# Side products held back in VectorE's queue, a fourth held weight chunk, and a hand-written end in a one-core transformer layer

## Chip, cores and metric

The kernel runs on one core of one Trainium2 chip, as one launch. The metric is the device time of an execution in microseconds (us), lower is better; of several runs the median counts.

## What is computed

One layer of a decoder trunk for 256 tokens of width 2048, all in float32. From the reference, cut to what matters here:

```python
mod = c_act @ w_mod[l] + b_mod[l]                    # one vector of 12288 per sequence
sh1, sc1, g1, sh2, sc2, g2 = jnp.split(mod, 6, axis=-1)
h = _rms_norm(x, mix_norm_pre[l]) * (1.0 + sc1[:, None]) + sh1[:, None]
y = _token_mixer(h, ...)                             # attention + gated linear attention, then @ w_out
x = x + g1[:, None] * _rms_norm(y, mix_norm_post[l])
h = _rms_norm(x, ffn_norm_pre[l]) * (1.0 + sc2[:, None]) + sh2[:, None]
y = _conv_ffn(h, ...)                                # w_up, causal convolution, gate, w_down
x = x + g2[:, None] * _rms_norm(y, ffn_norm_post[l])
```

`w_mod` is 2048 x 12288; it multiplies a single vector, so it is not a matmul of TensorE here but 96 x 2 multiply-and-sum passes of VectorE over tiles of 128 x 1024.

## The kernel before, in words

**Weights.** Every weight matrix is streamed once through SBUF in parts of 128 x 1024 float32 (512 KB). For each part q the program does four steps: `load` (SyncE starts the DMA into one of 4 `raw` buffers, four parts ahead), `prep` (ScalarE rounds `raw` into `hi`, L272; VectorE subtracts, `lo = raw - hi`, L276; three buffers of each), and three parts later the matmuls on `hi` and `lo` (`mm3` at L292 to L294, or the pair at L343). The product with `lo` keeps float32 accuracy, so TensorE cannot pass a part before VectorE's subtraction of it. I call L276 the subtraction.

**Side products.** The rows of `w_mod`, and the shift's share of the first projections, come through a second set of buffers, `auxb` (three, later two of 128 x 1024). `aux_load` (L239) starts their DMA on the same SyncE queue; `aux_proc` hands the tile to `mod_proc` (L207, one multiply-and-sum on VectorE, and a small L211 after each second one) or to `bias_proc`. The first 64 halves (`N_EARLY`) use other buffers. `aux_step` walks a list of due places, `pos`, and issues both.

**Order.** TensorE and SyncE run in the order in which the program is written (`manual_schedule` over the whole kernel). On VectorE, ScalarE and GpSimd a scheduler sets the order by its own estimate of when each instruction could start, except inside further `manual_schedule` blocks, where the order is the written one. So where a side product stands among the subtractions is the scheduler's choice.

**Output projection.** `outer_mm` keeps eight accumulators, two token halves t by four column blocks n, over 16 chunks c. With `split`, the last three chunks are multiplied for t = 0 first and their weights kept (`hold`, regions H and C), then for t = 1; so the norm of t = 0 runs beside the matmuls of t = 1. At a place in that second pass `mid` calls `h2_first`: the matmuls with a diagonal matrix (`h2_mm`, L1027) that transpose and scale x for the next layer half, and their evacuation. At the very end `evac_out` does the same for t = 1, with 52 dummy matmuls (`keep_warm`, L1020) while the chain of t = 1 runs: squares, sum and power -0.5 (`rstd4`, L940 and L941), the residual add (`out_x1`, L1000), squares again, `rstd4`, the diagonal (L120).

**End.** `evac_y2` finishes the second down projection: per block an add from PSUM (L1125), a square on ScalarE (L1126), the product with the gate row (L1120, on GpSimd for the first blocks, on VectorE for the others), and after the fourth block `rstd4` and four final multiply-adds (L1134), each with its output DMA (L1136).

Of the kernel before, what the change touches and what calls it, by code (L numbers as in the profile page):

```python
# [38 lines left out]
def block_kernel(ctx: ExitStack, tc: tile.TileContext, x, cvec, pos, idn, cst, vec, vec2, gmask,  # L39
# [190 lines left out]
    def aux_load(i):  # L230
# [24 lines left out]
    def prep(it, half, defer=False):  # L255
# [13 lines left out]
        else:  # L269
# [30 lines left out]
    def outer_mm(c, n_all, x_of, evac, split=False, mid=None):  # L300
# [13 lines left out]
        def go(it, half, hi, lo):  # L314
            if not split or c < n_all - 3:
                for n in (2 * half, 2 * half + 1):
                    for t in range(2):
                        one(c, t, n, hi, lo)
                return
# [3 lines left out]
            if c == n_all - 1 and half == 1:  # L323
                cs_ = range(n_all - 3, n_all)
# [619 lines left out]
    def evac_out(t, n, ps):  # L944
# [6 lines left out]
        if t == 0 or n < 3:  # L951
            out_sums(n, ps)
        if n < 3:
            return
        if t == 0:
            out_x1(0, rstd4(S["ss4"]))
            S["dg", 0] = diag_of(rstd4(S["ssx"]))
            return

        with tc.manual_schedule(engines={ET.DVE, ET.Activation}):  # L960
            out_sums(3, ps)
            up_lo = S["prep_up"]()
            h2_act(0, 2)
            rs = rstd4(S["ss4"])
            out_x1(1, rs)
            h2_act(0, 3)
            rs = rstd4(S["ssx"])
            h2_shift(0, 2)
            S["dg", 1] = diag_of(rs)
            h2_split(0, 2)  # L970
            h2_shift(0, 3)
            keep_warm()
            for n in range(4):
                h2_mm(1, n)
            h2_act(1, 0, range(1))
            h2_split(1, 0, range(1))
            h2_act(1, 0, range(1, 3))
            h2_shift(1, 0)
            h2_split(1, 0, range(1, 4))
            for n in range(1, 4):  # L980
                h2_act(1, n, range(4))
                h2_split(1, n)
                if n == 1:
                    up_lo()
                if n == 2:
                    h2_split(0, 3)
            S["prep_up"]()()

    def out_sums(n, ps):
        nc.scalar.activation(sqj, ps, AF.Square, accum_out=S["ss4"][:, n:n + 1])  # L990
        yg = t2k()
# [12 lines left out]
    def h2_first():  # L1004
# [6 lines left out]
        for n in range(2):  # L1011
            h2_act(0, n)
            h2_shift(0, n)
            h2_split(0, n)

    def keep_warm():

        wm = bank(4)
        for _ in range(52):
# [25 lines left out]
    def h2_split(t, n, js=range(4)):  # L1045
# [4 lines left out]
        nc.vector.tensor_copy(hh, ht)  # L1050
        nc.vector.tensor_tensor(hl, ht, hh.bitcast(F32), op=ALU.subtract)  # L1051
# [60 lines left out]
    def evac_y2(t, n, ps):  # L1112
        if n == 0:
            S["ss4"] = small(4, "ss4")
            S["yg"] = []
        y1 = S["y1"][:, t]

        def gate(m):
# [3 lines left out]
            S["yg"].append(yg)  # L1122
# [4 lines left out]
        gate(n)  # L1127
        if n < 3:
            return
        rs = rstd4(S["ss4"])  # L1130
        for n in range(4):
            ns = slice(n * 512, (n + 1) * 512)
            y = y1[:, ns]
            nc.vector.scalar_tensor_tensor(out=y, in0=S["yg"][n], scalar=rs, in1=S["x1"][:, t, ns], op0=ALU.mult,  # L1134
                                           op1=ALU.add)
            nc.sync.dma_start(out=out[t * P:(t + 1) * P, ns], in_=y)  # L1136
# [148 lines left out]
```

## Time and profile before

| what | value |
|---|---|
| median of 3 runs | 1598.68 us (1593.10, 1598.68, 1600.93) |
| the profiled execution's own time | 1597.75 us |
| its span, first to last instruction | 1595.6 us |
| TensorE busy | 1563.3 us, 98% |
| VectorE busy | 1222.5 us, 77% |
| ScalarE busy | 825.7 us, 52% |
| GpSimd busy | 17.0 us, 1% |
| mean granted TensorE clock | 0.997 |
| DMA | 403 MB, mean 253 GB/s |

The profiled execution's time is its span and 2.15 us around it. A matmul's end in the records is modelled and matmuls overlap, so TensorE's "busy" is an upper bound; its idle time between matmuls is what the views of waits show.

### The profile page before, as it was taken

Reading aid. Unit: us, or ns where it says so; the run is one execution under the profiler, and the core shown is the slowest. Engines: PE = TensorE matmul, PEld = TensorE weight load, DVE = VectorE, ACT = ScalarE, POOL = GpSimd, SP = SyncE. Lnnn points to the kernel's source line nnn. Section 1 sums busy time; section 2 is a strip of 40 time slices with the busy share of each in tenths; the row PEclk is TensorE's granted clock in tenths of the full one; section 3 lists DMA queues with packets and bytes.
Section 4 is the critical chain, followed back from the end, with each engine's and each line's share of the span. In section 5 each row is a group of like instructions: output and inputs, shape, how many; then the busy total and the mean of one; then the engine's idle time right before and its main releaser. Section 6 shows DMA issues by size and latency. Waiting matters only on the chain.

```text
span 1595.6 us, 21287 instructions
## 1 busy us (share of the span) xinstructions
PE 1563.3 (98%) x7752; PEld 1293.2 (81%) x7752; DVE 1222.5 (77%) x1869; ACT 825.7 (52%) x1221; POOL 17.0 (1%) x35
## 2 busy tenths in 40 slices
PE   8999999999999999999999999999999999999997
PEld 6878888877767788777888888888778888888886
DVE  7999989968977778877778877777546777776446
ACT  5455565544477544443366555555335555555333
POOL 0000000000000000000000000000000000000001
PEclk9999999999999999999999999999999999999999
DMA  9999987877777799889935667677665555555554
GB/s 367 382 352 410 360 274 257 277 273 256 250 244 263 257 306 326 293 293 314 354 133 199 230 231 238 217 245 231 231 224 187 182 185 185 186 186 189 194 197 132
DMA packets 154841, 403.18 MB, mean 253 GB/s; under 512 B 12720, under 2 KB 70704, under 8 KB 154480
## 3 DMA queue, kind: packets, MB, share of 16 engines
q1 hardware_dynamic: 154736, 401.82, 72.9%
q8 instruction: 61, 1.00, 0.3%
q14 instruction: 44, 0.36, 0.1%
HBM read 399.68 MB, written 2.10 MB: 252 GB/s over the span
## 4 chain that ended last, share of the span: by engine, by line
PE 31%; DMA 22%; DVE 13%; issue 5%; ACT 2%; SPq 1%; POOL 0%; DVEq 0%; POOLq 0%; ACTq 0%
DMA aux<-in_wM_dram 21%; PE ps L343 16%; DVE lo L276 6%; PE ps L293 5%; PE ps L294 5%; PE ps L292 5%; DVE aux L207 2%; DMA raw<-in_wO_dram 1%; ACT hi L272 1%; SPq L251 0%; DVE aux L348 0%; DVE t2k L742 0%; DVE t2k L1093 0%; DVE y L1134 0%; SPq L253 0%
## 5 line engine op out<-in xcount | busy, mean ns | idle before, releaser
L272 ACT CAST hi<-raw 128x1024 fp32r<-128x1024 f32 x520 | 544.9, 1050 | 476.1 <-PE ps L294 366.9
L276 DVE TENSOR_TENSOR lo<-raw,hi 128x1024 fp32r<-128x1024 f32 x518 | 629.2, 1221 | 142.0 <-ACT hi L272 139.6
L343 PE MATMUL ps<-h,hi 128*128 128x512 f32 x1664 | 582.0, 398 | 1.0 <-DVE h L1051 1.0
L343 PE MATMUL ps<-h,lo 128*128 128x256 f32 x1664 | 451.0, 281 | 1.0 <-DVE lo L276 0.9
L343 PEld LDWEIGHTS ps<-h,hi 128*128 128x128 f32 x1664 | 306.4, 188 | 69.2 <-issue 1.3
L343 PEld LDWEIGHTS ps<-h,lo 128*128 128x128 f32 x1664 | 314.0, 189 | 13.8 <-DVE lo L276 4.4
L207 DVE SCALAR_TENSOR_TENSOR aux<-aux,cact 128x1024 f32<-128x1024 f32 x128 | 156.4, 1223 | 145.7 <-DMA aux<-in_wM_dram 145.6
L292 PE MATMUL ps<-hi,h 128*128 128x512 f32 x608 | 240.0, 395 | 1.6 <-ACT h L297 1.1
L293 PE MATMUL ps<-lo,h 128*128 128x512 f32 x608 | 237.4, 391 | 2.6 <-DVE lo L276 2.5
L294 PE MATMUL ps<-hi,h 128*128 128x512 f32 x608 | 237.1, 390 | 1.5 <-DVE h L298 0.8
L293 PEld LDWEIGHTS ps<-lo,h 128*128 128x128 f32 x608 | 114.2, 188 | 29.2 <-DVE lo L276 4.9
L294 PEld LDWEIGHTS ps<-hi,h 128*128 128x128 f32 x608 | 114.1, 188 | 26.9 <-DVE h L298 1.2
L292 PEld LDWEIGHTS ps<-hi,h 128*128 128x128 f32 x608 | 114.2, 188 | 26.7 <-ACT h L297 1.5
L293 PE MATMUL ps<-lo,act_ab 128*128 128x512 f32 x256 | 100.3, 392 | 2.2 <-DVE lo L276 2.2
L294 PE MATMUL ps<-hi,act_ab 128*128 128x512 f32 x256 | 99.7, 389 | 0.0
L292 PE MATMUL ps<-hi,act_ab 128*128 128x512 f32 x256 | 99.7, 389 | 0.0
L207 DVE SCALAR_TENSOR_TENSOR early<-early,cact 128x1024 f32<-128x1024 f32 x64 | 78.0, 1218 | 1.3 <-ACT cact L143 1.3
L347 ACT ACTIVATE aux<-ps 128x256 f32<-128x256 f32 x88 | 33.5, 380 | 75.4 <-PE ps L343 75.2
L1090 ACT ACTIVATE t2k<-aux,vc 128x256 f32<-128x256 f32 x88 | 52.8, 601 | 26.6 <-DVE aux L348 26.4
L348 DVE SCALAR_TENSOR_TENSOR aux<-ps,aux 128x256 f32<-128x256 f32 x88 | 37.0, 421 | 35.6 <-ACT aux L347 35.6
L293 PEld LDWEIGHTS ps<-lo,act_ab 128*128 128x128 f32 x256 | 48.0, 188 | 14.4 <-DVE lo L276 4.6
L292 PEld LDWEIGHTS ps<-hi,act_ab 128*128 128x128 f32 x256 | 48.0, 188 | 10.1
(270 smaller groups left out, 1614.2 us busy)
## 6 DMA issues: line engine op xcount, KB each, us to landing
raw<-in_wU_dram SPq DMA_DIRECT2D x176, 512.0 KB, 3.8
aux<-in_wM_dram SPq DMA_DIRECT2D x128, 512.0 KB, 6.0
raw<-in_wD_dram SPq DMA_DIRECT2D x88, 512.0 KB, 3.9
early<-in_wM_dram SPq DMA_DIRECT2D x64, 512.0 KB, 6.7
raw<-in_wS_dram SPq DMA_DIRECT2D x32, 512.0 KB, 6.4
raw<-in_wOG_dram SPq DMA_DIRECT2D x32, 512.0 KB, 7.0
aux<-in_wS_dram SPq DMA_DIRECT2D x32, 512.0 KB, 5.7
raw<-in_wQK_dram SPq DMA_DIRECT2D x32, 512.0 KB, 5.4
```

The costliest lines, as they stand in the source:

```text
L207: nc.vector.scalar_tensor_tensor(out=raw, in0=raw, scalar=1.0, in1=cact[:, half * HW:(half + 1) * HW], op0=ALU.mult, op1=ALU.mult, accum_o ...
L272: nc.scalar.copy(hi[:, :w], raw)
L276: nc.vector.tensor_tensor(lo[:, :w], raw, hi[:, :w].bitcast(F32), op=ALU.subtract)
L292: nc.tensor.matmul(out=o, lhsT=lh, rhs=rh, start=start, stop=False)
L293: nc.tensor.matmul(out=o, lhsT=lh, rhs=rl, start=False, stop=False)
L294: nc.tensor.matmul(out=o, lhsT=ll, rhs=rh, start=False, stop=stop)
L343: nc.tensor.matmul(out=o, lhsT=w, rhs=m, start=c == 0 and o is ps, stop=c == nk - 1 and o is ps)
L347: nc.scalar.activation(o, ps[:, TOK:], AF.Copy, scale=scale)
L348: nc.vector.scalar_tensor_tensor(out=o, in0=ps[:, :TOK], scalar=scale, in1=o, op0=ALU.mult, op1=ALU.add)
L1090: nc.scalar.activation(z, u, AF.Identity, scale=w2, bias=vc2[:, W_CB + f:W_CB + f + 1])
```

## The change

Four edits; no arithmetic is added or taken away except six more dummy matmuls.

1. A side product beyond the first 64 is tied, by `tc.issue_after`, behind a subtraction on VectorE's queue: that of part lq + 3, where lq is the step at which the product's DMA was issued. That is the last weight part whose DMA stands ahead of the product's on SyncE's queue. It is an order on one engine's queue, without a semaphore.
2. The output projection holds its last four chunks instead of three; `mid` comes before the first block of the last chunk instead of before its third.
3. Behind `mid`, all of VectorE's and ScalarE's work up to the feed-forward layer is in written order, and that order is another: the four squares first, three gate products, the sum, the fourth gate product; `keep_warm` has 58 matmuls and writes bank 0 instead of 4.
4. The whole of `evac_y2` is in written order on VectorE, ScalarE and GpSimd: the four final multiply-adds of t = 0 are put between the blocks of t = 1 (one after block 0, one after block 1, two after block 2).

```diff
@@ aux_load, aux_proc
-        a["raw"] = raw
+        a["raw"], a["lq"] = raw, S.get("q", 0)
...
     def aux_proc(i):
         a = aux[i]
-        (mod_proc if a["kind"] == "mod" else bias_proc)(a, a["half"], a.pop("raw"))
+        go = mod_proc if a["kind"] == "mod" else bias_proc
+        if i < N_EARLY:
+            return go(a, a["half"], a.pop("raw"))
+
+        with tc.issue_after(los[max(k for k in los if k <= a["lq"] + LAG)]):
+            go(a, a["half"], a.pop("raw"))
@@ prep
-            nc.vector.tensor_tensor(lo[:, :w], raw, hi[:, :w].bitcast(F32), op=ALU.subtract)
+            los[it["q"] + half] = nc.vector.tensor_tensor(lo[:, :w], raw, hi[:, :w].bitcast(F32), op=ALU.subtract).ins
...
+    LAG, los = 3, {}
@@ outer_mm
-            if not split or c < n_all - 3:
+            if c < n_all - split:
...
-                    if n == 2 and c_ == n_all - 1 and mid:
+                    if n == 0 and c_ == n_all - 1 and mid:
                         mid()
@@ evac_out, t == 1
-        with tc.manual_schedule(engines={ET.DVE, ET.Activation}):
-            out_sums(3, ps)
-            up_lo = S["prep_up"]()
-            h2_act(0, 2)
-            rs = rstd4(S["ss4"])
-            out_x1(1, rs)
...
+        o = [S["o1", i] for i in range(4)]
+        for i in range(4):
+            out_square(i, o[i])
+        for i in range(3):
+            out_gate(i, o[i])
+        rs = rstd4(S["ss4"])
+        out_gate(3, o[3])
+        h2_act(0, 3)
+        out_x1(1, rs)
+        up_lo = S["prep_up"]()
...
@@ keep_warm
-        wm = bank(4)
-        for _ in range(52):
+        wm = bank(0)
+        for _ in range(58):
@@ items of wO
-        w_item(wO[c], D, outer_mm(c, KC, mg_of, evac_out, True, h2_first),
-               hold={KC - 3: ("H", True, 0), KC - 2: ("C", True, 0)}.get(c))
+        w_item(wO[c], D, outer_mm(c, KC, mg_of, evac_out, 4, h2_first),
+               hold={KC - 4: ("H", True, 0), KC - 3: ("H", False, 4), KC - 2: ("C", True, 0)}.get(c))
@@ evac_y2
+        if t == 0 and n == 0:
+            S["end"] = ExitStack()
+            S["end"].enter_context(tc.manual_schedule(engines={ET.DVE, ET.Activation, ET.Pool}))
+            S["out"] = []
...
         gate(n)
+        if t:
+
+            for _ in range((1, 1, 2, 0)[n]):
+                S["out"].pop(0)()
         if n < 3:
             return
         rs = rstd4(S["ss4"])
...
+        for m in range(4):
+            if t:
+                finish(m, rs)
+            else:
+                S["out"].append(lambda m=m: finish(m, rs))
```

Three places of the order show it. In these rows "aux" with its number is a side buffer, "macc" the product's sum, "lo<-raw,hi" a subtraction.

VectorE, where the first up projection ends and the first down projection begins; before:

```order
L298 TENSOR_TENSOR act_c<-t2k,act_c 128x256
L276 TENSOR_TENSOR lo<-raw,hi 128x1024 x2
L207 SCALAR_TENSOR_TENSOR aux_103,macc<-aux_103,cact 128x1024
L211 SCALAR_TENSOR_TENSOR modc<-macc,vc 128x1
L276 TENSOR_TENSOR lo<-raw,hi 128x1024 x4
L207 SCALAR_TENSOR_TENSOR aux_102,macc<-aux_102,cact 128x1024
```

and with the change:

```order
L304 TENSOR_TENSOR act_c<-t2k,act_c 128x256
L281 TENSOR_TENSOR lo<-raw,hi 128x1024
L207 SCALAR_TENSOR_TENSOR aux_102,macc<-aux_102,cact 128x1024
L281 TENSOR_TENSOR lo<-raw,hi 128x1024 x4
L207 SCALAR_TENSOR_TENSOR aux_103,macc<-aux_103,cact 128x1024
L211 SCALAR_TENSOR_TENSOR modc<-macc,vc 128x1
L281 TENSOR_TENSOR lo<-raw,hi 128x1024 x4
L207 SCALAR_TENSOR_TENSOR aux_102,macc<-aux_102,cact 128x1024
```

Each product stands two subtractions later. Counted over the whole program, 121 of the 160 side products that are tied stood, before, ahead of the subtraction of the last weight part requested before their own data; with the change none does.

VectorE, second unit of the sliding-window attention (dn is the softmax's denominator, es the sink's share, oa the attention's output); before:

```order
L276 TENSOR_TENSOR lo<-raw,hi 128x1024
L207 SCALAR_TENSOR_TENSOR aux_104,macc<-aux_104,cact 128x1024
L211 SCALAR_TENSOR_TENSOR modc<-macc,vc 128x1
L207 SCALAR_TENSOR_TENSOR aux_102,macc<-aux_102,cact 128x1024
L756 TENSOR_TENSOR dn<-dn,es 128x4
L757 RECIPROCAL dn<-dn 128x4
L207 SCALAR_TENSOR_TENSOR aux_103,macc<-aux_103,cact 128x1024
```

and with the change:

```order
L281 TENSOR_TENSOR lo<-raw,hi 128x1024
L207 SCALAR_TENSOR_TENSOR aux_102,macc<-aux_102,cact 128x1024
L207 SCALAR_TENSOR_TENSOR aux_103,macc<-aux_103,cact 128x1024
L211 SCALAR_TENSOR_TENSOR modc<-macc,vc 128x1
L762 TENSOR_TENSOR dn<-dn,es 128x4
L763 RECIPROCAL dn<-dn 128x4
L281 TENSOR_TENSOR lo<-raw,hi 128x1024 x2
```

Two products stand between the subtraction and dn in both, but not the same two: counted from the program's start, 121 side products stand ahead of this dn before, and 119 with the change. The 121st, of aux_102 right ahead of dn in the first excerpt, now comes after it.

VectorE, end of the program (y the down projection's output, x the residual); before:

```order
L1125 TENSOR_TENSOR y_10322<-ps_12722,y_10322 128x512
L1134 SCALAR_TENSOR_TENSOR y_10322<-t2k,r4r,x_6867 128x512 x4
L1125 TENSOR_TENSOR y_10322<-ps_12730,y_10322 128x512
L1125 TENSOR_TENSOR y_10322<-ps_12744,y_10322 128x512
L1125 TENSOR_TENSOR y_10322<-ps_12752,y_10322 128x512
L1120 TENSOR_TENSOR t2k<-y_10322,row 128x512
```

and with the change:

```order
L1162 TENSOR_TENSOR y_10324<-ps_12724,y_10324 128x512
L1157 SCALAR_TENSOR_TENSOR y_10324<-t2k,r4r,x_6851 128x512
L1162 TENSOR_TENSOR y_10324<-ps_12732,y_10324 128x512
L1157 SCALAR_TENSOR_TENSOR y_10324<-t2k,r4r,x_6851 128x512
L1162 TENSOR_TENSOR y_10324<-ps_12746,y_10324 128x512
L1157 SCALAR_TENSOR_TENSOR y_10324<-t2k,r4r,x_6851 128x512 x2
L1162 TENSOR_TENSOR y_10324<-ps_12754,y_10324 128x512
L1151 TENSOR_TENSOR t2k<-y_10324,row 128x512
```

The four final multiply-adds of t = 0 no longer stand in one block ahead of three of the four adds of t = 1, but between them.

## Rows read from the trace of the kernel before

**Rows 1.** Head of the page and its part 1.

```profile
span 1595.6 us, 21287 instructions
...
PE 1563.3 (98%) x7752; PEld 1293.2 (81%) x7752; DVE 1222.5 (77%) x1869; ACT 825.7 (52%) x1221; POOL 17.0 (1%) x35
```

**Rows 2.** TensorE's groups by line: xcount | busy us, mean ns | idle before, releasers.

```profile
L343 PE MATMUL ps<-h,lo 128*128 128x256 f32 x1664 | 451.0, 281 | 1.0 <-DVE lo L276 0.9
...
L293 PE MATMUL ps<-lo,h 128*128 128x512 f32 x608 | 237.4, 391 | 2.6 <-DVE lo L276 2.5
...
L293 PE MATMUL ps<-lo,act_ab 128*128 128x512 f32 x256 | 100.3, 392 | 2.2 <-DVE lo L276 2.2
...
L293 PE MATMUL ps<-lo,ob 128*128 128x512 f32 x128 | 50.2, 393 | 1.3 <-DVE lo L276 1.3
...
L293 PE MATMUL ps<-lo,mg 128*128 128x512 f32 x112 | 43.9, 392 | 0.8 <-DVE lo L276 0.8
...
L293 PE MATMUL ps<-lo,oa 128*128 128x512 f32 x64 | 25.3, 396 | 0.5 <-DVE lo L276 0.5
...
L783 PE MATMUL ps<-t2k,qkv 128*64 128x256 f32 (+1 forms) x40 | 8.2, 454 | 2.4 <-ACT t2k L772 2.4
```

**Rows 3.** Waits, all engines: us in total, times, longest.

```profile
DVE aux L207 <- DMA aux<-in_wM_dram: 145.6, 87, 4.5
```

**Rows 4.** VectorE's timeline, first down projection: start, us, line, idle before.

```profile
1120.42 1.23 DVE L207 SCALAR_TENSOR_TENSOR aux<-aux,cact 128x1024 f32<-128x1024 f32 x1 [4.49 <-DMA aux<-in_wM_dram]
...
1121.57 2.35 DVE L276 TENSOR_TENSOR lo<-raw,hi 128x1024 fp32r<-128x1024 f32 x2
```

**Rows 5.** TensorE's timeline there.

```profile
1122.85 0.50 PE L293 MATMUL ps<-lo,act_ab 128*128 128x512 f32 x1 [0.87 <-DVE lo L276]
```

**Rows 6.** VectorE's timeline, second unit of the attention.

```profile
467.04 1.22 DVE L207 SCALAR_TENSOR_TENSOR aux<-aux,cact 128x1024 f32<-128x1024 f32 x1 [3.30 <-DMA aux<-in_wM_dram]
...
468.19 0.16 DVE L756 TENSOR_TENSOR dn<-dn,es 128x4 f32<-128x4 f32 x1
```

**Rows 7.** ScalarE's timeline there.

```profile
466.56 0.60 ACT L834 ACTIVATE tb<-ps 128x512 f32<-128x512 f32 x1
...
468.66 1.70 ACT L760 ACTIVATE t2k<-t2k,dn 128x256 f32<-128x256 f32 x4 [1.50 <-DVE dn L757]
...
470.27 0.56 ACT L772 COPY t2k<-ps 128x512 f32<-128x512 f32 x1
```

**Rows 8.** Windows around it: busy by engine, granted clock (PEclk), DMA share, GB/s.

```profile
467.00:475.00 8.00, 5.62 (x19) 2.23 (x17) 5.90 (x10) 6.04 (x11) 0.00 (x0) 0.79 0.36 129
```

**Rows 9.** TensorE's timeline, end of the output projection.

```profile
823.50 3.84 PE L1027 MATMUL ps<-diag,x 128*128 128x128 f32 x32 [0.58 <-DVE diag L120]
...
828.56 6.38 PE L1020 MATMUL ps<-mg 128*128 128x256 f32 x52
...
836.12 3.81 PE L1027 MATMUL ps<-diag,x 128*128 128x128 f32 x32 [1.18 <-DVE diag L120]
...
843.48 0.47 PE L343 MATMUL ps<-h,hi 128*128 128x512 f32 x1 [0.61 <-DVE h L1051]
...
845.51 0.50 PE L343 MATMUL ps<-h,hi 128*128 128x512 f32 x1 [0.41 <-DVE h L1051]
```

**Rows 10.** VectorE's timeline, end of the program.

```profile
1580.91 3.84 DVE L1134 SCALAR_TENSOR_TENSOR y<-t2k,r4r,x 128x512 f32<-128x512 f32 x4
...
1586.58 0.72 DVE L1120 TENSOR_TENSOR t2k<-y,row 128x512 f32<-128x512 f32 x1
...
1588.96 2.74 DVE L1134 SCALAR_TENSOR_TENSOR y<-t2k,r4r,x 128x512 f32<-128x512 f32 x4 [1.09 <-POOL r4r L941]
```

**Rows 11.** GpSimd's timeline there.

```profile
1580.93 1.29 POOL L1120 TENSOR_TENSOR t2k<-y,row 128x512 f32<-128x512 f32 x1
...
1585.49 2.94 POOL L1120 TENSOR_TENSOR t2k<-y,row 128x512 f32<-128x512 f32 x2 [3.27 <-DVE y L1125]
...
1588.38 0.54 POOL L941 TENSOR_TENSOR r4r<-r4m,mhalf 128x1 f32<-128x1 f32 x1
```

More of the change, by code (lines that the diff above doesn't have):

```diff
@@ L298, in split_to, with outer_mm @@
         nc.vector.tensor_tensor(lo_ap, src_ap, hi_ap.bitcast(F32), op=ALU.subtract)
-    def outer_mm(c, n_all, x_of, evac, split=False, mid=None):
+    def outer_mm(c, n_all, x_of, evac, split=0, mid=None):
         def one(c, t, n, hi, lo):
@@ L323, in go @@
             if c == n_all - 1 and half == 1:
-                cs_ = range(n_all - 3, n_all)
+                cs_ = range(n_all - split, n_all)
                 for c_, n in [(c_, n) for c_ in cs_ for n in range(4)] if mid else [(c_, n) for n in range(4) for c_ in cs_]:
-                    if n == 2 and c_ == n_all - 1 and mid:
+                    if n == 0 and c_ == n_all - 1 and mid:
                         mid()
@@ new lines, in evac_out @@
+        keep_warm()
+        for n in range(4):
+            h2_mm(1, n)
+        up_lo()
+        h2_act(1, 0, range(1))
+        h2_split(1, 0, range(1))
+        h2_act(1, 0, range(1, 3))
+        h2_act(1, 0, range(3, 4))
+        h2_split(1, 0, range(1, 4))
+        h2_act(1, 1)
+        h2_shift(1, 1)
+        h2_split(1, 1)
+        up_lo = S["prep_up"]()
+        h2_act(1, 2, range(4))
+        h2_split(1, 2)
+        h2_act(1, 3)
+        h2_shift(1, 3)
+        h2_split(1, 3)
+        up_lo()
@@ L990, in out_sums, with out_square, out_gate @@
+        S["gap"].close()
+    def out_square(n, ps):
         nc.scalar.activation(sqj, ps, AF.Square, accum_out=S["ss4"][:, n:n + 1])
+    def out_gate(n, ps):
         yg = t2k()
@@ L1010, in h2_first @@
             h2_mm(0, n)
-        for n in range(2):
+        S["gap"] = ExitStack()
+        S["gap"].enter_context(tc.manual_schedule(engines={ET.DVE, ET.Activation}))
+        for n in range(3):
             h2_act(0, n)
             h2_shift(0, n)
-            h2_split(0, n)
+            if n < 2:
+                h2_split(0, n)
     def keep_warm():
-        wm = bank(4)
-        for _ in range(52):
+        wm = bank(0)
+        for _ in range(58):
             nc.tensor.matmul(out=wm[:, :TOK], lhsT=S["mgd"][0][:, 0, :P], rhs=S["mgd"][0][:, 0], start=True, stop=True)
@@ L1043, in h2_shift, with h2_halves @@
                                 scalar2=modc[:, 48 + c:49 + c], op0=ALU.mult, op1=ALU.add)
-    def h2_split(t, n, js=range(4)):
+    def h2_halves(t, n, js=range(4)):
         j0, j1 = js[0], js[-1] + 1
@@ L1049, in h2_split @@
         ht = S["h2t", t, n][:, j0 * P:j1 * P].rearrange("p (j t) -> p j t", t=P)
-        nc.vector.tensor_copy(hh, ht)
-        nc.vector.tensor_tensor(hl, ht, hh.bitcast(F32), op=ALU.subtract)
+        return (lambda: nc.vector.tensor_copy(hh, ht),
+                lambda: nc.vector.tensor_tensor(hl, ht, hh.bitcast(F32), op=ALU.subtract))
+    def h2_split(t, n, js=range(4)):
+        for part in h2_halves(t, n, js):
+            part()
     def mg_of():
@@ L1121, in gate, with finish @@
                                                                   op=ALU.mult)
-            S["yg"].append(yg)
+            ygs.append(yg)
+        def finish(m, rs):
+            ns = slice(m * 512, (m + 1) * 512)
+            nc.vector.scalar_tensor_tensor(out=y1[:, ns], in0=ygs[m], scalar=rs, in1=S["x1"][:, t, ns], op0=ALU.mult,
+                                           op1=ALU.add)
+            nc.sync.dma_start(out=out[t * P:(t + 1) * P, ns], in_=y1[:, ns])
         ns = slice(n * 512, (n + 1) * 512)
@@ L1130, in evac_y2 @@
         rs = rstd4(S["ss4"])
[L1131 to L1136, printed above, removed]
+        for m in range(4):
[3 more added lines that the diff above has]
+                S["out"].append(lambda m=m: finish(m, rs))
+        if t:
+            S["end"].close()
     N_PRE = len(aux)
@@ L1157, in block_kernel @@
         nh = -(-it["n"] // HW)
+        it["q"] = len(parts)
         parts += [(it, hf, hf == nh - 1) for hf in range(nh)]
```

49 lines of the change are left out of this document (18 added, 31 removed).

## The prediction

> **What bounds the kernel now.** I read the head of the page first: TensorE is busy 1563.3 of 1595.6 us [rows 1]. So the change can only win its idle time between matmuls and what stands ahead of its first matmul and behind its last: 32.3 us together. Nothing is won by making VectorE or ScalarE "less busy"; what counts is each place where TensorE stands still for them.
>
> Next come TensorE's groups with the idle time ahead of each and what ended it [rows 2]. Six of them, the matmuls with `lo` as operand, stood idle for 1.0 + 2.6 + 2.2 + 1.3 + 0.8 + 0.5 = 8.4 us, and nearly all of it was ended by the subtraction. One further group, the attention's product with the values (L783), waited 2.4 us for a copy of ScalarE.
>
> Why is the subtraction late, when VectorE is far from full? The list of waits says it: VectorE itself stood 145.6 us, in 87 waits, before a side product whose DMA had not landed [rows 3]. The timeline shows one such case whole. In the first down projection VectorE waits 4.49 us, runs the product (1.23 us), and only then two subtractions back to back [rows 4]; TensorE is held for 0.87 us and goes on as the first of the two is done [rows 5]. The weight parts for those two had been asked for before the product's data; the scheduler had merely put the product ahead. Most of the 145.6 us is covered by the three parts that lie ready; 8.4 us is what comes through.
>
> The attention shows the same in another coat. The product at 467.04 waited 3.30 us for its DMA with the tiny sum dn queued behind it [rows 6]; ScalarE, idle for 1.50 us, then scales (1.70 us) and copies [rows 7]; TensorE waits 2.4 us for that copy [rows 2], and in the 8 us around it the granted clock is 0.79, against 0.997 over the run [rows 8]: part of the stretch ran at the lower of the two levels (1.2 and 2.4 GHz), after TensorE had stood still.
>
> Two more places matter. At the end of the output projection TensorE waits 0.58 and 1.18 us for the diagonals and 0.61 and 0.41 us for the split of the next layer half, 2.78 us in all [rows 9]. Behind the last matmul there is a tail in which VectorE, ScalarE and GpSimd finish the output [rows 10, 11].
>
> **The change, part by part.** The sum is made against the profiled execution, 1597.75 us, which lies 0.93 us below the median of the three runs, 1598.68; I leave that difference alone.
>
> *Side products behind a subtraction, plain stages.* No work is added: 1.23 us per product as before. Tied to the last weight part requested ahead of it, a product can no longer wait for data younger than what the next subtraction in line needs. The ends of the price: all 8.4 us come back, or, since a product whose data is there still occupies VectorE for 1.23 us ahead of a subtraction [rows 4], some waits stay. In the order of the changed kernel, of the 17 places that make up the 8.4 us, 10 have lost the product that stood close ahead of the late subtraction; by the timeline they hold 4.4 us. At three (2.7 us) fewer instructions stand ahead, at four (1.3 us) the same. I take the 4.4 whole, 60% of the 2.7 and nothing of the rest: **-6.0 us**; ends -3 (most of the waits turn out to be DMA that is late anyway) and -8.4. The cover, if a product now lands late, is the same three ready parts; what would be late next is the load that reuses its buffer, the rival below.
>
> *The attention.* dn no longer has the 121st product ahead of it. It can then run as its own inputs end, ahead of ScalarE's sigmoid (until 467.16), so scaling and copy (1.70 and 0.56) follow directly: the copy ends near 469.4 instead of 470.83 [rows 7], some 1.3 us with the hand-over. If the stop is that short, the clock may hold: a shortfall of 0.21 over 8 us is 1.7 us of full clock [rows 8], of which I count 1.2 as matmul time. **-2.5 us**; ends 0 (dn is held by another product) and -3.6 (all of the 2.4 and the 1.2).
>
> *Output projection.* One more chunk in the second pass puts more matmuls of t = 1 between the end of t = 0 and the first diagonal: the 0.58 us can go. Moving `mid` ahead of all of the last chunk delays nothing on TensorE, but the t = 1 chain now begins after four blocks instead of two, and its long part (sum, power, four adds, four squares, sum, power, diagonal) is the same. Of the 1.18 us I expect about half from the fourth gate product, which now lies beside GpSimd's power; of the 1.02 us before the split, about a third. **-1.4 us**; ends -2.8 (all four waits) and +0.7: the dummies set a floor, 6 more of them at 6.38/52 = 0.12 us [rows 9], should the chain be ready early. The first held chunk also asks for the last weight parts sooner; I price that within these ends.
>
> *The written end.* With the four multiply-adds of t = 0 spread out, the add and square of each t = 1 block come when its matmuls are done. Without any clash GpSimd's two gate products would be over sooner, and the last power -0.5 would not start at 1588.38, right behind them [rows 11], but about 0.7 us earlier: -0.7. But the rows speak against it. The first group of four multiply-adds took 3.84 us, the last 2.74 [rows 10]; in the first a product of GpSimd ran at the same time (1580.93, 1.29 us), in the last none. And GpSimd's two products at 1585.49 took 2.94 us where two would be 2.58: VectorE's own gate product at 1586.58 lies inside [rows 10, 11]. So an operation of GpSimd and one of VectorE on two SBUF operands seem to exclude each other. Before, two of GpSimd's three products for t = 1 lay beside VectorE's adds from PSUM, where nothing collides; with the change they meet multiply-adds. One more collision costs up to 1.29 us, two 2.58. I take one less the part gained: **+1.0 us**; ends -0.7 and +2.3. The Trainium skill, SBUF — State Buffer, section "SBUF: two separate sides", says it outright: VectorE's and GpSimd's common port pair is "an exclusive lock, not a bandwidth split", held for the whole instruction, and it names VectorE operations with two SBUF inputs. The trace agrees (3.84 against 2.74 us); without that rule this term would be -0.7 and the sum 1.7 us lower.
>
> Sum: -6.0 - 2.5 - 1.4 + 1.0 = -8.9 us; 1597.75 - 8.9 = **1588.8 us**, 10 us (0.6%) below the median. A measurement of this kernel can tell about 0.5%, 8.0 us, from no change, so "faster" begins at 1590.7.
>
> **The rivals.**
>
> *Half of it (no change).* Landing is the limit, not place: the product waits as long, now with its successors behind it, and only the places without a product ahead gain. Then -3 for the side products, 0 in the attention, -0.7 and +1.5 at the two ends: 1595.5 us. For it speaks that 145.6 us of waiting is a lot of DMA that came late; against it, that in rows 4 the subtractions ran at once when the product was out of the way.
>
> *Buffers held longer (slower).* A product two subtractions later frees its buffer later; the load that reuses it stands on SyncE's queue ahead of the next weight load. It decides where the former product ends after the subtraction that the next weight load itself waits for. By the order that is so for 16 loads of the changed kernel (8 before). Each can push the weight loads by one product, 1.23 us: 16 x 1.23 = 20 us if nothing is ready to cover it, 1597.75 - 8.9 + 20 = 1609 us. Against it: in 61 more cases it is a tie that costs nothing, and three ready parts cover a single delay.
>
> *Everything comes back (faster).* All waits at their far ends, no collision: -8.4 - 3.6 - 2.8 - 0.7 = -15.5, 1582.2 us.
>
> **How the numbers follow.** Forecast, with 1584 to 1593 as its own spread from the ends above: 0.62, a quarter of it above 1590.7. Everything back: 0.10. Half: 0.22. Buffers: 0.06. Faster: 0.62 x 0.75 + 0.10 = 0.56; same: 0.155 + 0.22 = 0.38; slower 0.06. The range of 8 in 10 reaches down to the full gain and up to the half case: 1582 to 1596.
>
> **What would show it.** Right: VectorE's wait for the side loads falls from 145.6 to below 60 us, the six `lo` waits from 8.4 to about 2.4, the L783 wait below 1.2 us with the clock at 1.00 in that stretch, the first 0.58 us wait gone; at the end, longer multiply-adds beside GpSimd's products and a last power not earlier than now, counted from the last matmul. Wrong: `lo` waits that stay although the product is out of the way, weight casts of ScalarE waiting for DMA where they did not before, or a new wait of some microseconds at a stage change.

## The result and the profile after

The changed kernel takes **1579.19 us** (median of 4 runs, 1578.02 to 1580.28); the kernel before, with one more run beside it, 1599.81 us (4 runs, 1593.10 to 1602.13). The ratio is 0.9878, 95% interval 0.9846 to 0.9909: 1.2% faster, and 20.6 us between the medians. The forecast was 1588.8 us, range 1582 to 1596: right in sign, but outside the range; the gain is twice what was forecast. The profiled execution of after took 1580.28 us, 17.5 us less than the profiled one of before (spans 1578.1 and 1595.6 us, [rows 1]).

Head of the page of after:

```profile
span 1578.1 us, 21307 instructions
...
PE 1556.0 (99%) x7758; PEld 1296.4 (82%) x7758; DVE 1233.8 (78%) x1870; ACT 828.4 (52%) x1220; POOL 18.1 (1%) x35
```

Waits of TensorE after (us in total, times, longest); they answer to [rows 2] and [rows 9]:

```profile
PE ps L789 <- ACT t2k L778: 0.9, 1, 0.9
...
PE ps L1049 <- DVE diag L120: 0.7, 2, 0.4
...
PE ps L349 <- DVE lo L281: 0.2, 1, 0.2
PE ps L299 <- DVE lo L281: 0.2, 1, 0.2
```

The waits for `lo`, 8.4 us before, are down to 0.4. VectorE's group of side products shows why; it answers to [rows 3]:

```profile
L207 DVE SCALAR_TENSOR_TENSOR aux<-aux,cact 128x1024 f32<-128x1024 f32 x128 | 155.7, 1219 | 0.1
```

The same products at the same 1.22 us, but the idle time ahead of them is 0.1 us, where 145.6 us of waiting for the DMA stood. Not one tied product finds its data missing.

**Where the 17.5 us lie.** TensorE's matmuls come in the same order in both programs, but for the end of the output projection. So the start of the same matmul, by its number, can be compared in the two traces. The changed kernel's stretches, with the time that each became longer or shorter:

| stretch of after (us) | what runs there | change | forecast |
|---|---|---|---|
| 0 to 339 | first projections | +1.85 | 0 |
| 339 to 430 | projections and mixing ahead of the attention | -3.1 | side products |
| 430 to 511 | attention around L783 / L789 | -3.5 | -2.5 |
| 511 to 799 | the mixer's rest, plain part of the output projection | -7.95 | side products |
| 799 to 840 | end of the output projection | -0.9 | -1.4 |
| 840 to 1202 | first half of the feed-forward layer | -5.6 | side products |
| 1202 to 1566 | second half | 0.0 | 0 |
| behind the last matmul | the end | +1.7 | +1.0 |

They sum to -17.5; the medians are 20.6 apart, since the profiled execution of before lies 2.1 us below its median here and that of after 1.1 above. Of the +1.85, 1.65 is a slow stretch near 112 us (last section). The three stretches of the side products make -16.65 us, where -6.0 was forecast with ends of -3 and -8.4. The terms for the attention, the output projection and the end lie within their ends.

The attention, ScalarE's timeline, TensorE's and the window, answering to [rows 7], [rows 2] and [rows 8]:

```profile
465.47 1.69 ACT L766 ACTIVATE t2k<-t2k,dn 128x256 f32<-128x256 f32 x4
...
467.07 0.57 ACT L778 COPY t2k<-ps 128x512 f32<-128x512 f32 x1
```

```profile
467.69 1.07 PE L789 MATMUL ps<-t2k,qkv 128*64 128x512 f32 x2 [0.87 <-ACT t2k L778]
```

```profile
466.00:474.00 8.00, 7.13 (x32) 4.32 (x31) 5.39 (x12) 6.04 (x10) 0.00 (x0) 1.00 0.49 171
```

The scaling follows the sigmoid without the 1.50 us of idle time, TensorE stands 0.87 us instead of 2.4, and the granted clock stays at 1.00 where it was 0.79.

TensorE's timeline at the end of the output projection, answering to [rows 9]:

```profile
809.32 3.84 PE L1049 MATMUL ps<-diag,x 128*128 128x128 f32 x32 [0.45 <-DVE diag L120]
...
823.10 3.84 PE L1049 MATMUL ps<-diag,x 128*128 128x128 f32 x32 [0.24 <-DVE diag L120]
...
828.77 0.50 PE L349 MATMUL ps<-h,hi 128*128 128x512 f32 x1 [0.18 <-DVE h L1073]
```

And the end: the last matmul of TensorE, then VectorE and GpSimd, answering to [rows 10, 11]:

```profile
1566.15 0.39 PE L300 MATMUL ps<-hi,act_c 128*128 128x512 f32 x1
```

```profile
1562.66 1.85 DVE L1157 SCALAR_TENSOR_TENSOR y<-t2k,r4r,x 128x512 f32<-128x512 f32 x1
...
1566.30 2.84 DVE L1157 SCALAR_TENSOR_TENSOR y<-t2k,r4r,x 128x512 f32<-128x512 f32 x2
1569.06 0.68 DVE L1162 TENSOR_TENSOR y<-ps,y 128x512 f32<-128x512 f32 x1
...
1571.41 2.74 DVE L1157 SCALAR_TENSOR_TENSOR y<-t2k,r4r,x 128x512 f32<-128x512 f32 x4 [0.66 <-POOL r4r L947]
```

```profile
1565.26 3.33 POOL L1151 TENSOR_TENSOR t2k<-y,row 128x512 f32<-128x512 f32 x2 [1.29 <-DVE y L1162]
1570.83 0.55 POOL L947 TENSOR_TENSOR r4r<-r4m,mhalf 128x1 f32<-128x1 f32 x1 [2.24 <-DVE r4j L946]
```

The last block's add (1569.06) is 2.5 us behind the last matmul's end (1566.15 + 0.39), because it stands in the written order behind two multiply-adds that take 2.84 us beside GpSimd's products, where two alone take some 1.4 (half of the last group's 2.74).

### The profile page after: what moved, and what is told of

The parts are those of the page before. It is cut to its first block, busy times and chain, and to the rows that moved or that the text cites. A ratio compares the mean times of both kernels' runs of the same rounds, so it can differ in the third digit from the quotient of the medians.

```text
span 1578.1 us, 21307 instructions
## 1 busy us (share of the span) xinstructions
PE 1556.0 (99%) x7758; PEld 1296.4 (82%) x7758; DVE 1233.8 (78%) x1870; ACT 828.4 (52%) x1220; POOL 18.1 (1%) x35
## 4 chain that ended last, share of the span: by engine, by line
PE 69%; DVE 3%; ACT 1%; issue 1%; POOL 0%; DVEq 0%; POOLq 0%; ACTq 0%
PE ps L349 31%; PE ps L298 12%; PE ps L299 12%; PE ps L300 12%; DVE lo L281 1%; PE ps L742 0%; PE ps L789 0%; ACT aux L1021 0%; PE ps L775 0%; DVE aux L207 0%; DVE y L1157 0%; PE ps L1049 0%; PE ps L921 0%; DVE t2k L1011 0%; DVE y L1162 0%
## 5 line engine op out<-in xcount | busy, mean ns | idle before, releaser
L299 PEld LDWEIGHTS ps<-lo,act_ab 128*128 128x128 f32 x256 | 48.1, 188 | 10.1
L300 PEld LDWEIGHTS ps<-hi,act_ab 128*128 128x128 f32 x256 | 48.0, 188 | 9.9
L298 PEld LDWEIGHTS ps<-hi,act_ab 128*128 128x128 f32 x256 | 48.0, 188 | 9.9
```

The lines of the kernel that those rows point to most:

```text
L298: nc.tensor.matmul(out=o, lhsT=lh, rhs=rh, start=start, stop=False)
L299: nc.tensor.matmul(out=o, lhsT=lh, rhs=rl, start=False, stop=False)
L300: nc.tensor.matmul(out=o, lhsT=ll, rhs=rh, start=False, stop=stop)
```

## Why the waits were worth twice their idle time

Before any experiment the old trace could answer this. Its waits, by engine; the second and third row are those of the weight loads (PEld):

```profile
PE ps L293 <- DVE lo L276: 7.4, 12, 1.4
...
PEld ps L293 <- DVE lo L276: 15.6, 23, 1.8
...
PEld ps L343 <- DVE lo L276: 4.4, 10, 0.8
```

TensorE itself shows a wait for `lo` at 15 places (12 for L293, 3 for L343), but its weight loads waited at 33. Two of these places in TensorE's timeline of before. The first is that of [rows 5], whose own row stands between the two:

```profile
1121.59 0.39 PE L292 MATMUL ps<-hi,act_ab 128*128 128x512 f32 x1
...
1123.18 0.40 PE L294 MATMUL ps<-hi,act_ab 128*128 128x512 f32 x1
```

Matmuls of this shape normally start 0.23 us apart. Here 1.26 us lie between 1121.59 and 1122.85, so 1.03 are lost where the row says 0.87; and 0.33 us lie before the next, 0.10 more. The stop cost 1.13 us.

The second place shows no idle time in TensorE's rows at all (TensorE, then the weight load):

```profile
953.93 0.63 PE L343 MATMUL ps<-h,hi 128*128 128x512 f32 x2
954.50 0.38 PE L343 MATMUL ps<-h,lo 128*128 128x256 f32 x1
954.72 0.40 PE L343 MATMUL ps<-h,hi 128*128 128x512 f32 x1
```

```profile
954.50 0.19 PEld L343 LDWEIGHTS ps<-h,lo 128*128 128x128 f32 x1 [0.38 <-DVE lo L276]
```

The same matmuls after:

```profile
934.88 0.63 PE L349 MATMUL ps<-h,hi 128*128 128x512 f32 x2
935.35 0.28 PE L349 MATMUL ps<-h,lo 128*128 128x256 f32 x1
935.46 0.40 PE L349 MATMUL ps<-h,hi 128*128 128x512 f32 x1
```

From the first row to the third it is 0.79 us before and 0.58 after: 0.21 us lost, without a row that says so, because the recorded ends, which are modelled, leave no gap there.

Counted over all matmuls of the three stretches of the side products, start to start, before against after, the 16.65 us are: 11.1 at 17 late subtractions (8.3 us of idle time by the waits and some 0.16 us of restart at each); 3.8 in 37 intervals that are 20 to 150 ns too long, each within 0.4 us of a weight load that waited for `lo`; 1.7 at four stops for other operands that VectorE makes; 0.1 in the rest.

## The experiments

In the comparisons below the kernel before took 1610 to 1613 us, on four chips; the variants are told apart against each other and by the stages of their traces.

**The ties alone**, in the kernel before: edit 1 of the change and none of the others.

```diff
+        with tc.issue_after(los[max(k for k in los if k <= a["lq"] + LAG)]):
+            go(a, a["half"], a.pop("raw"))
```

> The kernel before with the ties of the side products alone. Theory A: the ties carry the whole gain, and the prediction's term for them was too small because it counted TensorE's idle time at six groups, where each late subtraction also costs a restart and many short delays. Aligned matmul by matmul, the two traces give -16.7 us for the plain stages and -3.5 us for the attention. So about 20 us less than the kernel before in the comparison, 1578 to 1582 us, and the idle time ahead of the matmuls that take lo below 1 us. Theory B: the ties bring the 8.5 us that the prediction gave them, and the rest comes from the chunks held at the output projection and their order, which moves everything behind it: about 1591 us.

Measured: 1578.24 us (6 runs, 1577.78 to 1580.19), ratio to the kernel before 0.9806 (0.9779 to 0.9833). The last matmul of its profiled execution, and two waits of TensorE:

```profile
1567.72 0.39 PE L300 MATMUL ps<-hi,act_c 128*128 128x512 f32 x1
```

```profile
PE ps L1033 <- DVE diag L120: 1.8, 2, 1.2
PE ps L349 <- DVE h L1057: 1.0, 2, 0.6
```

Theory A holds: one edit of four gives all of the gain. The old waits at the end of the output projection (1.8 and 1.0) are still there, and the span ends 9.9 us behind the last matmul, as before. Against the changed kernel it needs 1.5 us more from the attention to the feed-forward layer, and its end is 1.7 us shorter: the other three edits cancel.

**Without the ties**: the changed kernel, edits 2 to 4 only.

```diff
-        with tc.issue_after(los[max(k for k in los if k <= a["lq"] + LAG)]):
-            go(a, a["half"], a.pop("raw"))
+        go(a, a["half"], a.pop("raw"))
```

> The changed kernel with the ties taken out; the fourth held chunk, the written order at the output projection and the written end stay. Theory A: the output projection brings about -0.8 us (the difference of the two traces across it) and the end +1.7 us, so no gain: 0 to 2 us more than the kernel before. Theory B: half of the gain is here, some 8 to 11 us less than the kernel before.

Measured: 1610.51 us against 1610.73, ratio 1.0007 (0.9984 to 1.0030). No gain, as theory A has it. Its waits:

```profile
DVE aux L207 <- DMA aux<-in_wM_dram: 144.3, 87, 4.9
```

```profile
PE ps L295 <- DVE lo L277: 13.1, 16, 1.5
```

The wait is as long as before (145.6 us in 87, [rows 3]); what of it reaches TensorE is more in this execution. Its tail is 10.5 us, where theory A had 11.6: the last block's add starts 1.5 us behind the last matmul instead of 2.5. So by this profile what the written end costs also depends on when TensorE is done.

**The former end**: the changed kernel with `evac_y2` of the kernel before.

```diff
-        if t:
-            for _ in range((1, 1, 2, 0)[n]):
-                S["out"].pop(0)()
...
-        for m in range(4):
-            if t:
-                finish(m, rs)
-            else:
-                S["out"].append(lambda m=m: finish(m, rs))
+        for n in range(4):
+            nc.vector.scalar_tensor_tensor(out=y, in0=S["yg"][n], scalar=rs, in1=S["x1"][:, t, ns], op0=ALU.mult,
+                                           op1=ALU.add)
...
```

> The changed kernel with the former end. In the traces the span ends 11.6 us behind the last matmul with the change and 9.9 us before. Theory A: the written end costs that difference, so this run is 1.7 us shorter than the changed kernel, near 1577.5 us, with some 9.9 us behind the last matmul. Rival: the tail is longer for something else (the run's own scatter), or the last matmul itself ends earlier for the written order: then the time is that of the changed kernel, or more, 1579 to 1581 us.

Measured: 1578.87 us (1577.29 to 1579.81). In the profile the last matmul starts at 1565.17 and the span is 1575.4 us: 9.8 us behind its end. The tail is the expected one. The medians show 0.3 us of it and do not resolve it: single runs of either kernel differ by up to 2.5 us. The two profiles differ by 1.6 us in the stretch that the last section names.

**More work behind the ties**: 80 further operations on VectorE.

```diff
         with tc.issue_after(los[max(k for k in los if k <= a["lq"] + LAG)]):
+            r = a["raw"]
+            if i % 2:
+                nc.vector.scalar_tensor_tensor(out=r, in0=r, scalar=1.0, in1=r, op0=ALU.mult, op1=ALU.max)
             go(a, a["half"], a.pop("raw"))
```

> The changed kernel with one more operation of the same size on VectorE ahead of every second tied product (out = max(x, x) over the loaded half, 80 times some 1.22 us, 98 us of VectorE's time). Theory A: VectorE's time behind the subtraction costs nothing, only the place and the wait ahead of it did: within 3 us of the changed kernel, 1578 to 1582 us. Rival C (buffers held longer, the slower rival of the prediction): each such operation holds the side buffer 1.22 us longer, and the load that reuses it stands on SyncE's queue ahead of a weight load; if the three ready parts do not cover that, some tens of us more, 1600 us or above. A result between would say that VectorE is nearly full in some stages.

Measured: 1591.39 us, 12 us more than the changed kernel: between the two. By matmul starts 9 of them arise between 230 and 340 us. The window there, of this kernel and of the changed one (span, then busy time of PE, PEld, DVE, ACT, POOL, granted clock, DMA share, GB/s):

```profile
230.00:340.00 110.00, 103.59 (x562) 86.66 (x561) 105.45 (x161) 54.13 (x85) 0.21 (x1) 0.98 0.72 244
```

```profile
230.00:340.00 110.00, 110.00 (x606) 92.89 (x606) 100.87 (x161) 60.13 (x94) 0.91 (x2) 1.00 0.82 276
```

VectorE, at 100.9 of 110 us already, is nearly full in this stage with the additions (105.5). But the buffers are held longer too: in this window ScalarE's casts wait 17.7 us for weights, which they do not in the changed kernel, and over the program SyncE stands 117 us before side loads for their buffers, where it stood 38. The run does not separate the two. Of the 80, 53 run behind 471 us, and there their 64 us of VectorE's time cost 2.5 us. So a product's own 1.22 us is nearly free where VectorE has room; the price in [rows 2] was that of its waiting. (Another 3.4 us are lost between 408 and 430 us; 1.9 come back in the attention, as in the next run.)

**Ties one subtraction earlier.**

```diff
-    LAG, los = 3, {}
+    LAG, los = 2, {}
```

> The changed kernel with each side product tied one subtraction earlier: in VectorE's queue 98 products of 160 now stand one place ahead of the last weight part requested before their data, 62 at or behind it (changed kernel: all at or behind it; before: 121 ahead, most of them by two). Theory A (the price is the wait for data that was asked for after the next subtraction's weights): part of VectorE's 144 us of waiting for these transfers comes back, and with it part of the gain; as one place is half of the two that most products stood ahead before, 1585 to 1595 us. Rival D (the gain comes from a fixed order, whichever it is): as the changed kernel, 1578 to 1580 us.

Measured: 1576.50 us (1575.72 to 1578.18). Theory A's number is missed, and rival D's too: it is slightly faster. VectorE's wait, and the table loads of ScalarE for the sigmoid here and in the changed kernel:

```profile
DVE aux L207 <- DMA aux<-in_wM_dram: 2.5, 3, 1.4
```

```profile
L840 ACT ACT_TABLE_LOAD x3 | 3.8, 1283 | 0.1
```

```profile
L840 ACT ACT_TABLE_LOAD x4 | 5.1, 1283 | 0.1
```

One place earlier still leaves the data time to land: 2.5 us of waiting. Of the 2.7 us between the medians, 1.9 arise between 449 and 471 us, in the attention; the profiles further differ by the stretch of the last section (1.65 us). There the moved products let the scheduler put ScalarE's exponentials and sigmoids in groups; it loads its tables 10 instead of 12 times in the program (1.28 us each), the copy for L789 starts at 462.79 instead of 467.07, and the 0.87 us wait is gone. By the timelines it is an effect of ScalarE's order, not of VectorE's; no run changed ScalarE's order alone.

**Two subtractions earlier.**

```diff
-    LAG, los = 3, {}
+    LAG, los = 1, {}
```

> The changed kernel with each side product tied two subtractions earlier: 101 of 160 products stand two places ahead of the last weight part requested before their data, as most did before the change, but the order is fixed by the tie. One place ahead cost nothing (2.5 us of waiting for these transfers, 1576.5 us). Theory A (the price is VectorE's wait for the transfer): the slack is now used up, as before the change; VectorE waits 100 us or more for the transfers again, and the time is that of the kernel before, 1598 to 1612 us. Rival D (a fixed order is what brings it): 1577 to 1582 us.

Measured: 1604.21 us (12 runs, 1599.74 to 1608.67), ratio 0.9956 (0.9939 to 0.9974). Its waits:

```profile
DVE aux L207 <- DMA aux<-in_wM_dram: 133.5, 75, 5.3
```

```profile
PE ps L299 <- DVE lo L281: 10.6, 14, 1.9
PE ps L349 <- DVE lo L281: 5.1, 6, 1.5
```

Theory A holds and rival D falls: with ties in place but the products two places ahead, the 133.5 us and the late subtractions are back. The price is the wait for the transfer, and it sets in sharply: nothing at one place ahead, 25 us against the changed kernel at two, of the 32 by which the kernel before is longer beside it. An estimate says why: a place is one weight part, some 3 us (518 casts in 1578 us), and the side transfers land 5.9 us after their issue (median, page of after), which is two parts.

**Two subtractions later.**

```diff
-    LAG, los = 3, {}
+    LAG, los = 5, {}
```

> The changed kernel with each side product tied two subtractions later (98 products now stand two places behind the last weight part requested before their data, 60 one place). No work is added. Theory A: the data had landed anyway, so nothing is won, and a buffer that is freed some 4 us later costs nothing while three weight parts lie ready: 1578 to 1581 us; then the 12 us that the extra operations cost were VectorE's time in its full stages, not the buffers. Rival C (buffers held longer): the loads that reuse the side buffers come later and hold the weight loads behind them on SyncE's queue: 1585 us or more, and ScalarE's casts wait longer for weights than the 27 us of the changed kernel.

Measured: 1586.62 us (1583.97 to 1586.83), 7.4 us more than the changed kernel. Rival C is real here. SyncE's waits in this kernel, and the same row in the changed one:

```profile
SPq L239 <- DVE aux L207: 200.8, 64, 8.3
```

```profile
SPq L239 <- DVE aux L207: 38.0, 34, 4.2
```

SyncE stands before the side loads until their buffers come free, and the weight loads stand behind it. ScalarE's casts wait 64 us for weights (sum over its rows); the changed kernel has 27 and 36 in its two profiles, and the other kernels with `LAG` 2 or 3 up to 45 where nothing was added. 6.4 us of the loss arise between 709 and 776 us. There one cast waits 8.2 us for its weights (longest in the changed kernel 4.6), and TensorE stands for that cast, a wait that the changed kernel does not have:

```profile
PE ps L298 <- ACT hi L277: 2.2, 1, 2.2
```

The tie of the change sits between two costs: two places later the buffers cost, two places earlier the data do.

**Another spread of the end**: the changed kernel with 1, 1, 1, 1 and the last gate product behind the sum.

```diff
-        gate(n)
-        if t:
-            for _ in range((1, 1, 2, 0)[n]):
-                S["out"].pop(0)()
+        if t:
+            S["out"].pop(0)()
         if n < 3:
+            gate(n)
             return
         rs = rstd4(S["ss4"])
+        gate(n)
```

> The changed kernel; at the end one multiply-add of t = 0 behind each block of t = 1 instead of 1, 1, 2, 0, and the last gate product behind the sum of squares, where VectorE waits for the power. In the changed kernel VectorE reaches the last block's add 2.5 us behind the last matmul, because it stands behind two multiply-adds that overlap GpSimd's gate products (1.16 and 1.74 us instead of 0.75). If the place is the cause, the add comes some 1.6 us earlier and the gate product (0.7) drops out of the path: 9.5 to 10.3 us behind the last matmul instead of 11.6, as the former end. If the stretching by GpSimd sets it wherever the operation stands, 11 us or more.

Measured: 1578.24 us (1577.29 to 1580.30); in the profile the span (1575.8) ends 10.1 us behind the last matmul's end (1565.70). As expected for the place: the last add starts 0.6 us behind the last matmul instead of 2.5. The stretching stays: three of the four multiply-adds of t = 0 still take 1.2 us each beside GpSimd.

**An end without overlaps**: GpSimd keeps only gate products that lie beside adds from PSUM.

```diff
-            (nc.gpsimd if m < 2 + t else nc.vector).tensor_tensor(yg, y1[:, m * 512:(m + 1) * 512], row("g2r", m),
+            (nc.gpsimd if m < 2 and m >= t else nc.vector).tensor_tensor(yg, y1[:, m * 512:(m + 1) * 512], row("g2r", m),
...
-        gate(n)
-        if t:
-            for _ in range((1, 1, 2, 0)[n]):
+        if n < 2:
+            gate(n)
+        if t and n == 0:
+            while S["out"]:
                 S["out"].pop(0)()
         if n < 3:
             return
+        gate(2)
         rs = rstd4(S["ss4"])
+        gate(3)
```

> The changed kernel with another end: GpSimd keeps only the gate products that lie beside VectorE's adds from PSUM (two for t = 0, one for t = 1); the four multiply-adds of t = 0 stand together behind the first block of t = 1, and the last two gate products stand behind the last add, one of them where VectorE waits for the power. If VectorE and GpSimd exclude each other on operations with two SBUF operands, no multiply-add is stretched now, all eight take some 0.74 us, and the last add starts at the last matmul's end: 8.5 to 9.3 us behind the last matmul, against 11.6 in the changed kernel and 9.8 with the former end; the whole time 1575 to 1577.5 us. If the exclusion is not the cause, the three gate products more on VectorE (0.7 us each) show as a longer tail, 10.5 us or more.

Measured: 1576.93 us (1576.05 to 1578.05). Last matmul, and VectorE's timeline behind it:

```profile
1566.46 0.39 PE L300 MATMUL ps<-hi,act_c 128*128 128x512 f32 x1
```

```profile
1563.88 1.41 DVE L1157 SCALAR_TENSOR_TENSOR y<-t2k,r4r,x 128x512 f32<-128x512 f32 x2
...
1566.89 0.69 DVE L1162 TENSOR_TENSOR y<-ps,y 128x512 f32<-128x512 f32 x1 [0.41 <-PE ps L300]
...
1569.64 2.74 DVE L1157 SCALAR_TENSOR_TENSOR y<-t2k,r4r,x 128x512 f32<-128x512 f32 x4 [0.44 <-POOL r4r L947]
```

The add starts 0.04 us behind the last matmul's end, the multiply-adds take 0.74 us again, and the span (1576.3) ends 9.45 us behind the matmul, just above the expected 8.5 to 9.3, 2.1 us less than with the change and 0.4 less than with the former end. VectorE now does two gate products more (the expectation says three; GpSimd goes from five to three) and is done sooner. The Trainium skill, SBUF — State Buffer, section "SBUF: two separate sides", calls the port pair of the two engines an exclusive lock; the runs agree (1.85 us for the overlapped multiply-add at 1562.66, 0.74 without a product beside it).

**Both together**: the ties one subtraction earlier and the end without overlaps, both diffs in one kernel.

> The changed kernel with the ties one subtraction earlier, as in the run that was 2.5 us shorter, and with the end in which GpSimd keeps only three gate products. The two act in different places, the attention near 470 us and the stretch behind the last matmul. If they add: 2.0 us from the attention and 2.1 us from the end (11.6 to 9.45 us), 1574 to 1575.5 us, less than each alone. If the last stretch depends on where the earlier work leaves VectorE: 1576 to 1577 us.

Measured: 1575.91 us (6 runs, 1573.97 to 1576.09). That lies between the two expectations, so it was run again beside the changed kernel.

**The changed kernel again, and both together again**, on one chip.

> The changed kernel again, on the chip of this comparison. In the comparisons with the variants the kernel before took 1610 to 1612 us (1599.8 in the first comparison), while the variant with the ties alone took 1578.2. Theory A (the ties cut TensorE loose from the moment at which the side data land): the changed kernel takes 1578 to 1581 us here too, whatever the kernel before takes. Rival E (the other chip is slower by its transfers, and all kernels with it): its time rises with that of the kernel before, by some 10 us, to 1588 to 1591 us.

> The kernel with the ties one subtraction earlier and the other end again, beside the changed kernel on the same chip. By the stages of the profiles it is 1.9 us shorter near the attention and 2.1 us at the end: 3 to 4.5 us less than the changed kernel in the same call. If the gain is the scatter of one slow stretch near 112 us, which some executions of every kernel show (1.6 us), less than 1.5 us.

Measured: the changed kernel 1578.78 us (1577.75 to 1580.20), the other 1574.33 us (1574.07 to 1576.19), the kernel before 1613.35 us; ratios 0.9791 (0.9773 to 0.9809) and 0.9765 (0.9747 to 0.9783). Theory A holds: the changed kernel's time is that of the first comparison to 0.4 us, while the kernel before is 13.5 us longer. The other kernel is 4.4 us shorter, well above the 1.5 us that would have been scatter and at the upper end of what was expected. By the traces it is 1.9 us shorter in the attention and 2.2 behind the last matmul, and 0.8 longer between 511 and 845 us. So the two repairs add, and this is the fastest version of this study; the 4.4 us itself hold some of the scatter that the last section shows.

## Why the prediction was right and wrong

- **What bounds the kernel**: half right. The products that waited for their DMA were the cause (ties alone 0.9806, without them 1.0007). But the first step allowed the change only TensorE's idle time, 32.3 us, and that was wrong: from before to after the idle time fell by 10.2 us (to 22.1), and TensorE's busy time by 7.3 (1563.3 to 1556.0). A matmul behind a late weight load can show as a longer one, as that at 954.50 (0.38 us, 0.28 after).
- **"Side products behind a subtraction, plain stages", -6.0 us**: this step failed; it measured -16.65. The `lo` waits, of which it left 2.4 us, fell to 0.4. Three things went wrong in it. It took the price from the idle time of the six groups, 8.4 us, and made that the far end; but a late weight load also costs a restart and delays too short for a wait row, so late subtractions held about 15 us (11.1 and 3.8). It then gave back 2.4 us for places where the product still stood near, as if a product cost by its 1.23 us; the run with 80 more operations shows that 53 of them cost 2.5 us together, and the ties took the waiting alone away. And it left out other results of VectorE, 1.7 us.
- **Attention, -2.5 us**: right in mechanism, -3.5 measured, near its far end of -3.6. The wait fell to 0.87 us (below 1.2, as written down), and the clock stayed up.
- **Output projection, -1.4 us**: -0.9 measured by matmul starts. The 0.58 us wait, which was to be gone, is 0.45; the other three fell further than thought (1.18 to 0.24, 0.61 to 0.18, 0.41 to 0.08). Of the first of these three falls, 0.94 us, the six added dummies fill some 0.7 (58 take 7.11 us, 52 took 6.38), so less was won than the waits say.
- **Written end, +1.0 us**: right in sign, +1.7 measured, within its ends, and right in cause in part. The collision is one part; the other, which the step did not have, is that the last block's add now waits behind it in the written order. With another spread the add comes 0.6 us behind the last matmul and the tail is 10.1 us, though the collision stays.
- **Half of it**: excluded. Landing was not the limit; VectorE's wait went from 145.6 to 0.1 us.
- **Buffers held longer**: did not happen at the place that was chosen, but two places later it costs 7.4 us, by the mechanism described. It was a rival with the right mechanism and the wrong point of onset.
- **Everything comes back, 1582.2 us**: nearest to the result of all the stated cases, and still too small, since its far end for the side products was 8.4 us. Its nearness is in part luck: it had -0.7 us for the written end, where +1.7 was measured.

What stays open: why the kernel before is 10 to 14 us slower on the chips of the experiments. Its weight transfers landed later there (medians of the untied run 4.2 and 4.8 us for the two feed-forward matrices, against 3.8 and 3.9 before), and a transfer that is later could make VectorE wait longer. But the untied run's profile shows no longer wait (144.3 us against 145.6), and the ties alone ran as fast with 4.7 us for both. No run varied the transfers by themselves.

## What to carry over

Price a late operand by the start-to-start times of the matmuls and by the waits of the weight loads, not by TensorE's idle rows: here late subtractions with 8.3 us of idle time were worth 15. In an in-order queue, put an operation that reads a transfer behind whatever depends on older transfers only; one part earlier was still free here, two parts earlier cost 25 us, two parts later 7. A written order at the end paid here, by 0.4 us, only where the operations on which two engines exclude each other were taken apart first.

## What was not expected of the hardware

**A stretch of low clock that comes and goes.** The changed kernel lost 1.6 us near 112 us, at eight matmuls that each took 0.2 us more. The window of after and that of before:

```profile
111.00:118.00 7.00, 7.00 (x25) 5.59 (x24) 6.96 (x13) 3.23 (x6) 0.00 (x0) 0.76 0.99 313
```

```profile
111.00:118.00 7.00, 7.00 (x33) 5.78 (x32) 6.96 (x14) 3.36 (x6) 0.00 (x0) 1.00 0.95 299
```

The mean granted clock is 0.76 in one and 1.00 in the other: a part of the 7 us ran at 1.2 instead of 2.4 GHz. In both TensorE had stood idle just before, for about 1.0 and 0.8 us between 107 and 110 us. Of the 14 profiles five show a clock below 1.00 here (0.76 to 0.81) and nine do not; the changed kernel and the fastest version were profiled twice each, and each shows both (0.76 and 1.00, 0.77 and 1.00). The 11 executions of the fastest version lie near 1574.1 us (five) or 1576.0 us (six); the profiled one with 1.00 took 1573.97, the one with 0.77 1576.12. So the same stop lowers the clock in one execution and not in the next, and 1.6 us of difference between two tied kernels say nothing until this window has been looked at.

**How steady a kernel becomes.** The kernel before took between 1593 and 1619 us over all its runs; every kernel with `LAG` 2 or 3 stayed within 2.2 us of its own median, on whatever chip it ran. That fits products which, while they wait for their data, carry the time of each transfer into the result; no run varied the transfers to show it.
